# Weight tiles and attention operands moved to other addresses modulo 512 bytes in a one-core encoder block

## The chip, the cores and the metric

One core of a Trainium2 chip runs the whole block in one launch. The metric is the device time of that launch in microseconds. The engines are PE (TensorE: matmuls, with its weight loads listed apart as PEld), DVE (VectorE), ACT (ScalarE), POOL (GpSimd) and SP (SyncE, which issues DMAs here).

## The reference

A hybrid streaming-encoder block on x (1, 512, 1024) and a memory mem (1, 256, 1024), all in float32:

```python
h = rms_norm(x, norm_mix_g)
proj = h @ w_in + b_in
y_a = rwkv7_branch(proj[..., :cb0], ...) @ w_branch_a     # delta-rule recurrence, 8 heads of 64
y_b = rglru_branch(proj[..., cb0:cb1], proj[..., cb1:cb2], ...) @ w_branch_b
merged = sigmoid(proj[..., cb2:cg1]) * y_a + sigmoid(proj[..., cg1:]) * y_b
x = x + merged @ w_mix_out
x = x + cross_attention(rms_norm(x), rms_norm(mem), w_cq, w_ckv, w_co)   # 4 heads of 256
x = x + conv_ffn(rms_norm(x), w_ffn_in, conv, w_ffn_out)                 # d_ff = 2816, causal conv of 3
return rms_norm(x, norm_final_g)
```

## The kernel before, in words

**Three matmuls for one product.** Weights and activations are float32. Each is split into a high part, rounded to the type float32r, and a low part, the rest; a product is high x high, high x low and low x high, summed in PSUM (`mm3`, lines 165 to 169). The weight is always the stationary operand but for the V projection, where the memory is. Line 166 multiplies the high weight with the high activation, line 167 the high weight with the low activation, line 168 the low weight with the high activation. PE loads the weight anew for each of the three.

**Weight tiles.** Weights come from DRAM in tiles of 128 partitions x 1024 float32, that is eight units of 128 x 128. SP issues the load of a tile into a raw tile (tag `wr`, four buffers), ACT casts it to the high part (tag `wh`, three buffers), DVE subtracts to get the low part (tag `wl`, three buffers). `stream` (lines 100 to 122) does so for the dense layers, `stream_quarters` (124 to 135) for the first FFN layer, `out_weights` (1315 to 1343) for the second. Each of them allocates `wh` first and `wl` second.

**Stages, in the order of PE's work.** K projection of the memory (`k_ps`, 256 columns), V projection (`v_ps`), the input projection in 38 blocks (`in_ps`, 512 columns), interleaved with the chunked recurrence of small matmuls; the two branch outputs (`yb_ps`, `ya_ps`, four units a block and eight blocks each), the mix (`mix_ps`), the queries (`q_ps`) interleaved with the attention (`sc_ps`, `prT_ps`, `o_ps`), its output (`co_ps`); then the FFN in a form that needs seven products of half size in place of eight (quarters A11, s1, s2, s4, s3, A12, A22, each 256 columns wide). FFN in runs 11 blocks x 7 products x 2 tiles of 128 rows x 4 units (`fx_ps`, `fyz_ps`); FFN out runs 7 products x 4 rows of tiles x 11 units (`ox_ps`, `oyz_ps`). The sums of weight quarters that this form needs are made by accumulating DMAs on POOL's queue (lines 482 and 518), paced by PE.

**Where the tiles lie.** An address here is a tile's byte offset within a partition, as the program allocates it. Pools lie behind one another. The weight pool comes first, at 16,512: four raw tiles, three high, three low, 4,096 bytes each. The constant pool `cp` follows at 57,472, with `ones` (float32) and `onesr` (float32r) among its tiles, 512 bytes each; then the pool `big` at 65,984, which holds most activations; then, from 115,136, the pools of each stage. Since a unit of weights has 512 bytes and a slice of an activation 1,024 or 2,048, every slice of a tile has the remainder modulo 512 that the tile has:

| tile | role | address mod 512 |
|---|---|---|
| raw, high and low weights | loaded; stationary (moving in the V projection) | 128 |
| h, merged, branch outputs, FFN operands | moving | 448 |
| m2 (the memory) | moving for K, stationary for V | 448 |
| o2 (attention output) | moving for `co_ps` | 0 |
| K2, probabilities prT | moving in the attention | 0 |
| q2, V2 | stationary in the attention | 0 |

The pool `pb` starts with `rxc` and `nrx` (four floats each, 32 bytes taken each: lines 1056 and 1057), which puts o2 behind them at 0 modulo 512 (line 1068).

**The start.** DVE fills `ones` (line 209) and casts it to `onesr` (line 212); eleven matmuls on `onesr` (line 288) wake PE. `ones` serves the float32 sums of squares (lines 271, 338, 1062, 1394), `onesr` the split ones.

**Order.** Weight loads are issued by SP in the order of use, as buffers come free; a high-priority block puts the casts ahead of other work on ACT and DVE. `rxc`, the per-row scale of the scores, is made by `rsqrt` and `newton` (lines 1063 to 1066) from `ssx`, and read by the Exp of the scores (line 1116).

Of the kernel before, what the change touches and what calls it, by code (L numbers as in the profile page):

```python
# [9 lines left out]
F32 = mybir.dt.float32  # L10
F32R = mybir.dt.float32r
# [6 lines left out]
P = 128  # L18
T = 512
D = 1024  # L20
KB = D // P
NMEM = 256
# [36 lines left out]
def hybrid_block_kernel(ctx: ExitStack, tc: tile.TileContext, xT_d, mT_d, pv_d, cst_d, win_d, wk_d, wv_d,  # L59
                        lup_d, gup_d, rga_d, rgx_d, wba_d, wbb_d, wmix_d, wq_d, wo_d, wfi_d, wfo_d, out_d):  # L60
    nc = tc.nc
    V, S, PE = nc.vector, nc.scalar, nc.tensor

    wp = ctx.enter_context(tc.tile_pool(name="wp", bufs=3))
    cp = ctx.enter_context(tc.tile_pool(name="cp", bufs=1))
# [12 lines left out]
    def rw_ps(name, pool=None, tag="rw", **kw):  # L78
        return (pool or prw).tile([P, T], F32, tag=tag, name=name, **kw)
# [16 lines left out]


    wdma, mdma, casts = [], [], []

    def stream(dram, name, between=None, order=None):  # L100

        for g in order or range(dram.shape[0]):
            with tc.high_priority():
                raw = wp.tile([P, 1024], F32, tag="wr", name=f"{name}_r{g}", bufs=4)
                n = 512 if len(wdma) < 2 else 1024
                ins = nc.sync.dma_start(raw, dram[g])
                if between is not None:
                    tc.keep_in_program_order(ins)
                    between(0)
                elif len(wdma) == 1:  # L110
                    tc.add_manual_dep(ins.ins, mdma[-1].ins.name, mybir.DependencyInfo(
                        mybir.DependencyClass.NoSync, mybir.DependencyReason.DATA), reason="order of the loads")
                wdma.append(ins)
                hi = wp.tile([P, 1024], F32R, tag="wh", name=f"{name}_h{g}")
                lo = wp.tile([P, 1024], F32R, tag="wl", name=f"{name}_l{g}")
                for o in range(0, 1024, n):
                    casts.append(S.copy(hi[:, o:o + n], raw[:, o:o + n]))  # L117
                    V.tensor_tensor(lo[:, o:o + n], raw[:, o:o + n], hi[:, o:o + n].bitcast(F32), ALU.subtract)  # L118
                    if between is not None and o == 0:
                        between(1)  # L120
                between = None
            yield hi, lo

    def stream_quarters(srcs, name):

        for g, src in enumerate(srcs):
            with tc.high_priority():
                raw = wp.tile([P, 2, T], F32, tag="wr", name=f"{name}_r{g}", bufs=4)
                wdma.append(nc.sync.dma_start(raw, src))
                hi = wp.tile([P, 2, T], F32R, tag="wh", name=f"{name}_h{g}")  # L130
                lo = wp.tile([P, 2, T], F32R, tag="wl", name=f"{name}_l{g}")
                S.copy(hi, raw)  # L132
                V.tensor_tensor(lo, raw, hi.bitcast(F32), ALU.subtract)  # L133
            for i in range(2):
                yield hi[:, i], lo[:, i]

    class Units:
# [10 lines left out]
        def next(self):  # L148
            if self.left == 0:
                self.fill()  # L150
            i = self.i
            self.i += 1
            self.left -= 1
            return self.hi[:, i * P:(i + 1) * P], self.lo[:, i * P:(i + 1) * P]
# [50 lines left out]


    eps = cp.tile([P, 4], F32, name="eps")
    ones = cp.tile([P, P], F32, name="ones")
    V.memset(ones, 1.0)
    bonesr = cp.tile([P, P], F32R, name="bonesr")  # L210
    onesr = cp.tile([P, P], F32R, name="onesr")
    V.tensor_copy(onesr, ones)
    V.memset(eps[:, 0:1], 1e-6)
    V.memset(eps[:, 1:2], 64e-5)
    V.memset(eps[:, 2:3], 1e-30)
# [67 lines left out]
    with tc.tile_pool(name="p0", bufs=1, reuse_waits="tile") as p0:  # L283
# [103 lines left out]
        for hf in range(2):  # L387
            pss = [(mm_ps if hf else rw_ps)(f"v_ps{hf}_{i}") for i in range(2)]
            for k2 in range(4):
                wh, wl = next(st)  # L390
# [108 lines left out]
    def out_units(m, r, c):  # L499

        return [divmod(((r - 1) * MQ + m) * FB + (c - 1) * HB + k, 8) for k in range(HB)]
# [236 lines left out]
    with tc.tile_pool(name="pz", bufs=1, reuse_waits="tile") as pz:  # L738
# [9 lines left out]
        for s in range(30, -1, -1):  # L748
            n = 31 - s
# [303 lines left out]

    pb_ctx = ExitStack()
    pb = pb_ctx.enter_context(tc.tile_pool(name="pb", bufs=1, reuse_waits="tile"))
    rxc = pb.tile([P, 4], F32, name="rxc")
    nrx = pb.tile([P, 4], F32, name="nrx")
    pat_ctx = ExitStack()
    pat = pat_ctx.enter_context(tc.tile_pool(name="pat", bufs=1, space=PSUM, reuse_waits="tile"))
    psc = rw_ps("rxc_ps", pat, "sc", bufs=2)  # L1060
# [4 lines left out]
    V.tensor_scalar(rxc, rxc, 1.0 / 16, None, ALU.mult)  # L1065
    V.tensor_scalar(nrx, rxc, -1.0, None, ALU.mult)

    o2 = pb.tile([P, 2, KB, T], F32R, name="o2")
    pk_ctx = ExitStack()
    pk = pk_ctx.enter_context(tc.tile_pool(name="pk", bufs=1, reuse_waits="tile"))  # L1070
    K2 = pk.tile([P, 2, KB, NMEM], F32R, name="K2")
    V2 = pk.tile([P, 2, 2, D], F32R, name="V2")

    def load_kv(what, i):
        kv = pk.tile([P, D], F32, tag="kv", name=f"kv{what}{i}", bufs=KVB)
        if what == "K":
            ks = slice(4 * i, 4 * i + 4)
            hi, lo = K2[:, 0, ks], K2[:, 1, ks]
            kv = kv.rearrange("p (m n) -> p m n", n=NMEM)
# [19 lines left out]
        return q2  # L1099

    def attend(hd, q2):
        prT = pk.tile([P, 2, 2, T], F32R, tag="prT", name=f"prT{hd}", bufs=2)
        prps = [rw_ps(f"prT_ps{hd}_{i}", pat, "prT", bufs=2) for i in range(2)]
        for tt in range(4):
            sl = slice(tt * P, (tt + 1) * P)
            ps = rw_ps(f"sc_ps{hd}_{tt}", pat, "sc", bufs=2)
            for i in range(2):
                kb = 2 * hd + i
                PE.matmul(ps[:, :NMEM], q2[:, 0, i, sl], K2[:, 0, kb, :], start=(i == 0), stop=False)
                PE.matmul(ps[:, :NMEM], q2[:, 0, i, sl], K2[:, 1, kb, :], start=False, stop=False)  # L1110
                PE.matmul(ps[:, :NMEM], q2[:, 1, i, sl], K2[:, 0, kb, :], start=False, stop=(i == 1))
            st = pk.tile([P, 4], F32, tag="smst", name=f"smst{hd}_{tt}", bufs=4)
            V.tensor_reduce(st[:, 0:1], ps[:, :NMEM], AX.X, ALU.max)
            V.tensor_tensor(st[:, 1:2], st[:, 0:1], nrx[:, tt:tt + 1], ALU.mult)
            ex = pk.tile([P, NMEM], F32, tag="ex", name=f"ex{hd}_{tt}", bufs=3)
            S.activation(ex, ps[:, :NMEM], AF.Exp, scale=rxc[:, tt:tt + 1], bias=st[:, 1:2],
                         accum_out=st[:, 2:3])
            V.reciprocal(st[:, 3:4], st[:, 2:3])
            V.tensor_scalar(ex, ex, st[:, 3:4], None, ALU.mult)
            for i in range(2):  # L1120
                PE.transpose(prps[i][:, sl], ex[:, i * P:(i + 1) * P], ident)
        for i in range(2):
            S.copy(prT[:, 0, i, :], prps[i])
            V.tensor_tensor(prT[:, 1, i, :], prps[i], prT[:, 0, i, :].bitcast(F32), ALU.subtract)
        for i in range(2):
            kb = 2 * hd + i
            ps = rw_ps(f"o_ps{kb}", pat, "o")
            for n in range(2):
                cs = slice(kb * P, (kb + 1) * P)
                mm3(ps, V2[:, 0, n, cs], V2[:, 1, n, cs], prT[:, 0, n, :], prT[:, 1, n, :], n == 0, n == 1)  # L1130
            S.copy(o2[:, 0, kb, :], ps)
            V.tensor_tensor(o2[:, 1, kb, :], ps, o2[:, 0, kb, :].bitcast(F32), ALU.subtract)
# [36 lines left out]
    for m in order:  # L1169
# [3 lines left out]
        h = ph.tile([P, T], F32, tag=f"h{m // 4}", name=f"h{m}")  # L1173
        S.activation(h, xr[:, m, :], AF.Identity, scale=par("nffn", m))
        i = m % 4
# [139 lines left out]
    def out_weights():  # L1315

        flat = []
        for n in ("A11", "A12", "s1", "s2", "s3", "A22", "s4"):
            for m, k in out_order:
                if n[0] == "A":  # L1320
                    p, i = out_units(m, int(n[1]), int(n[2]))[k]
                    flat.append((p, wfo_d[p], i))
                else:
                    flat.append(((n, m), dO["s2" if n == "s4" else n, m], k))
        for g in range(0, len(flat), 8):
            units = flat[g:g + 8]
            n = len(units) * P
            with tc.high_priority():
                raw = wp.tile([P, 1024], F32, tag="wr", name=f"wfo_r{g // 8}", bufs=4)
                k = 0  # L1330
                while k < len(units):
                    key, src, i = units[k]
                    e = k
                    while e < len(units) and units[e][0] == key and units[e][2] == i + e - k:
                        e += 1
                    nc.sync.dma_start(raw[:, k * P:e * P], src[:, i * P:(i + e - k) * P])
                    k = e
                hi = wp.tile([P, 1024], F32R, tag="wh", name=f"wfo_h{g // 8}")
                lo = wp.tile([P, 1024], F32R, tag="wl", name=f"wfo_l{g // 8}")
                S.copy(hi[:, :n], raw[:, :n])  # L1340
                V.tensor_tensor(lo[:, :n], raw[:, :n], hi[:, :n].bitcast(F32), ALU.subtract)  # L1341
            for k in range(len(units)):
                yield hi[:, k * P:(k + 1) * P], lo[:, k * P:(k + 1) * P]
# [186 lines left out]
```

## Time and profile before

| what | value |
|---|---|
| median of 3 runs | 894.85 us (892.56 to 897.15) |
| span of the profiled execution | 892.8 us |
| mean granted TensorE clock | 0.996 |
| PE busy | 877.4 us, 6197 matmul records |
| weight loads busy | 767.9 us |
| DVE busy | 685.2 us |
| ACT busy | 513.6 us |
| moved by DMA | 201.37 MB |

A row of the timeline has the start in us from the span's start, the duration in us, the engine, the line, the operation, output and inputs, and the shape. Matmuls are pipelined: the duration is the latency of one, and the next starts long before it ends, so a rate is read from starts. A row of waits names who waited, for whom, the total, how often, and the longest. A row of the windows view has, for a stretch of time, the sum and the busy time (and count) of PE, PEld, DVE, ACT and POOL, then the granted clock, the share of the DMA engines and GB/s.

### The profile page before, as it was taken

What the parts mean: (1) busy time and instruction counts of PE and PEld (TensorE: products, weight loads), DVE (VectorE), ACT (ScalarE), POOL (GpSimd) and SP (SyncE); (2) the same over time, 40 slices, a digit from 0 to 9 for tenths busy, and PEclk for the clock granted to TensorE, in tenths of its full rate; (3) what the DMA queues carried; (4) which work ended last, traced back from release to release, by engine and by line L of the source; (5) the groups of instructions that cost most, each with busy time, mean ns of one, the idle gap of its engine ahead of it and who ended that gap; (6) DMA issues with size and microseconds to landing.
All of it is one profiled execution on the core that took longest, in us unless ns stands there. A gap on an engine that the chain in (4) does not pass through costs nothing.

```text
span 892.8 us, 15934 instructions
## 1 busy us (share of the span) xinstructions
PE 877.4 (98%) x6197; PEld 767.9 (86%) x6197; DVE 685.2 (77%) x1104; ACT 513.6 (58%) x783; POOL 132.5 (15%) x163
## 2 busy tenths in 40 slices
PE   8999999999999999999999999999999999999996
PEld 7878878888877677888888778999999999999996
DVE  6796598777967677675575578889888889999674
ACT  6575676634347676233554466766655656757563
POOL 0101222021102021001122111111111111211100
PEclk9999999999999999999999999999999999999999
DMA  7878899678997279758888958999999999998963
GB/s 268 307 253 215 206 228 233 187 203 233 262 227 156 72 203 249 220 166 229 218 234 183 197 137 185 260 275 271 265 255 294 263 297 275 244 276 220 261 202 94
DMA packets 97242, 201.37 MB, mean 226 GB/s; under 512 B 19536, under 2 KB 30928, under 8 KB 97104
## 3 DMA queue, kind: packets, MB, share of 16 engines
q1 hardware_dynamic: 62240, 118.57, 40.4%
q0 software_dynamic: 25504, 67.38, 36.9%
q10 hardware_dynamic: 9424, 14.42, 4.7%
q8 instruction: 48, 0.79, 0.4%
q14 instruction: 26, 0.21, 0.1%
HBM read 188.54 MB, written 78.12 MB: 299 GB/s over the span
## 4 chain that ended last, share of the span: by engine, by line
PE 91%; DVE 4%; DMA 2%; ACT 1%; issue 1%; DVEq 0%; ACTq 0%; SPq 0%
PE in_ps L167 7%; PE in_ps L166 7%; PE in_ps L168 7%; PE fx_ps L167 5%; PE fx_ps L166 5%; PE fx_ps L168 5%; PE fyz_ps L167 4%; PE fyz_ps L166 4%; PE fyz_ps L168 3%; PE ox_ps L166 2%; PE oyz_ps L166 2%; PE ox_ps L168 2%; PE oyz_ps L168 2%; PE oyz_ps L167 2%; PE ox_ps L167 2%; PE co_ps L167 2%
## 5 line engine op out<-in xcount | busy, mean ns | idle before, releaser
L132 ACT CAST wfi_h<-wfi_r 128x1024 fp32r<-128x1024 f32 x77 | 81.1, 1053 | 71.5 <-PE fx_ps L167 19.7
L168 PE MATMUL in_ps<-hT,win_l 128*128 128x512 f32 x304 | 121.3, 399 | 0.0
L167 PE MATMUL in_ps<-hT,win_h 128*128 128x512 f32 x304 | 121.0, 398 | 0.2 <-DVE hT L384 0.2
L166 PE MATMUL in_ps<-hT,win_h 128*128 128x512 f32 x304 | 120.6, 398 | 0.3 <-DVE pr L586 0.3
L133 DVE TENSOR_TENSOR wfi_l<-wfi_r,wfi_h 128x1024 fp32r<-128x1024 f32 x77 | 94.1, 1222 | 22.7 <-ACT wfi_h L132 22.4
L482 POOL DMA_DIRECT2D dS<-in_wfi x66 | 66.7, 1028 | 293.1 <-PE in_ps L166 102.3
L167 PEld LDWEIGHTS in_ps<-hT,win_h 128*128 128x128 f32 x304 | 57.1, 188 | 14.2 <-issue 0.7
L166 PEld LDWEIGHTS in_ps<-hT,win_h 128*128 128x128 f32 x304 | 57.1, 188 | 13.2 <-DVE pr L586 0.7
L168 PEld LDWEIGHTS in_ps<-hT,win_l 128*128 128x128 f32 x304 | 57.1, 188 | 13.1 <-issue 0.7
L518 POOL DMA_DIRECT2D dOs<-in_wfo x54 | 39.8, 784 | 181.5 <-PE fyz_ps L166 54.0
L118 DVE TENSOR_TENSOR win_l<-win_r,win_h 128x1024 fp32r<-128x1024 f32 x38 | 46.3, 1221 | 24.2 <-ACT win_h L117 20.7
L117 ACT CAST win_h<-win_r 128x1024 fp32r<-128x1024 f32 x38 | 39.9, 1050 | 41.1 <-PE in_ps L167 32.4
L1341 DVE TENSOR_TENSOR wfo_l<-wfo_r,wfo_h 128x1024 fp32r<-128x1024 f32 (+1 forms) x39 | 47.2, 1209 | 15.2 <-ACT wfo_h L1340 15.2
L1340 ACT CAST wfo_h<-wfo_r 128x1024 fp32r<-128x1024 f32 (+1 forms) x39 | 40.5, 1039 | 31.3 <-DMA wfo_r<-dOs 11.6
L168 PE MATMUL ox_ps<-go,wfo_l 128*128 128x256 f32 x176 | 49.1, 279 | 0.8 <-DVE wfo_l L1341 0.8
L166 PE MATMUL ox_ps<-go,wfo_h 128*128 128x256 f32 x176 | 49.2, 279 | 0.4 <-ACT wfo_h L1340 0.3
L166 PE MATMUL fx_ps<-hq,wfi_h 128*128 128x256 f32 x176 | 49.4, 280 | 0.0
L166 PE MATMUL fyz_ps<-hq,wfi_h 128*128 128x256 f32 x176 | 49.2, 280 | 0.0
L167 PE MATMUL fx_ps<-hq,wfi_h 128*128 128x256 f32 x176 | 49.2, 280 | 0.0
L167 PE MATMUL fyz_ps<-hq,wfi_h 128*128 128x256 f32 x176 | 49.2, 280 | 0.0
L167 PE MATMUL fx_ps<-hr,wfi_h 128*128 128x256 f32 x176 | 49.2, 280 | 0.0
L166 PE MATMUL fx_ps<-hr,wfi_h 128*128 128x256 f32 x176 | 49.2, 279 | 0.0
(432 smaller groups left out, 2704.9 us busy)
## 6 DMA issues: line engine op xcount, KB each, us to landing
dS<-in_wfi POOLq DMA_DIRECT2D x66, 512.0 KB, 7.8
wfi_r<-dS SPq DMA_DIRECT2D x44, 512.0 KB, 6.8
win_r<-in_win SPq DMA_DIRECT2D x38, 512.0 KB, 5.3
wfi_r<-in_wfi SPq DMA_DIRECT2D x33, 512.0 KB, 5.8
dS<-dS POOLq DMA_DIRECT2D x22, 512.0 KB, 5.7
dOs<-in_wfo POOLq DMA_DIRECT2D x12, 512.0 KB, 7.9
wk_r<-in_wk SPq DMA_DIRECT2D x8, 512.0 KB, 5.1
wv_r<-in_wv SPq DMA_DIRECT2D x8, 512.0 KB, 4.0
```

What stands on the lines that cost most here:

```text
L117: casts.append(S.copy(hi[:, o:o + n], raw[:, o:o + n]))
L118: V.tensor_tensor(lo[:, o:o + n], raw[:, o:o + n], hi[:, o:o + n].bitcast(F32), ALU.subtract)
L132: S.copy(hi, raw)
L133: V.tensor_tensor(lo, raw, hi.bitcast(F32), ALU.subtract)
L166: first = PE.matmul(ps, lh, rh, start=start, stop=False, **kw)
L167: PE.matmul(ps, lh, rl, start=False, stop=False, **kw)
L168: PE.matmul(ps, ll, rh, start=False, stop=stop, **kw)
L482: return lambda: nc.gpsimd.dma_start(s(out), src, **kw)
L518: yield lambda k=k, w=w, src=src: nc.gpsimd.dma_start(dO[n, m][:, k * P:(k + w) * P], src, **kw)
L1340: S.copy(hi[:, :n], raw[:, :n])
L1341: V.tensor_tensor(lo[:, :n], raw[:, :n], hi[:, :n].bitcast(F32), ALU.subtract)
```

## The change

The three places that allocate a high and a low weight tile call a new function, which allocates the low tile first. Three pads are put into the weight pool: 128 bytes ahead of the raw tiles, 128 bytes between the low and the high tiles, 256 bytes behind the high ones. Raw tiles then lie at 256, low parts at 256, high parts at 384 modulo 512, and the pools behind start 512 bytes later.

`ones` is no longer a tile of its own: it is `onesr` read as float32, and DVE writes 1.0 straight into it. The constant pool is 512 bytes shorter, so `big` and all behind it lie where they were.

In the attention o2 is the first tile of its pool, K2 and the two buffers of probabilities follow, and `rxc` and `nrx` become slices of one tile behind them. o2, K2 and the probabilities then lie at 448 modulo 512, V2 and q2 at 0 as before.

No instruction of the loops is added or taken away; one cast at the start goes.

```diff
+    wp.tile([P, 32], F32, name="pad_r", bufs=1)
+    pads = iter(((32, "pad_h"), (64, "pad_e")))
+
+    def weight_tiles(name, g):
+
+        t = {}
+        for i in "lh":
+            t[i] = wp.tile([P, 1024], F32R, tag=f"w{i}", name=f"{name}_{i}{g}")
+            for n, pad in islice(pads, 1):
+                wp.tile([P, n], F32, name=pad, bufs=1)
+        return t["h"], t["l"]
...
-                hi = wp.tile([P, 1024], F32R, tag="wh", name=f"{name}_h{g}")
-                lo = wp.tile([P, 1024], F32R, tag="wl", name=f"{name}_l{g}")
+                hi, lo = weight_tiles(name, g)
...
-                hi = wp.tile([P, 2, T], F32R, tag="wh", name=f"{name}_h{g}")
-                lo = wp.tile([P, 2, T], F32R, tag="wl", name=f"{name}_l{g}")
+                hi, lo = (t.rearrange("p (n f) -> p n f", n=2) for t in weight_tiles(name, g))
...
-    ones = cp.tile([P, P], F32, name="ones")
-    V.memset(ones, 1.0)
     bonesr = cp.tile([P, P], F32R, name="bonesr")
     onesr = cp.tile([P, P], F32R, name="onesr")
-    V.tensor_copy(onesr, ones)
+    ones = onesr.bitcast(F32)
+    V.memset(ones, 1.0)
...
-    rxc = pb.tile([P, 4], F32, name="rxc")
-    nrx = pb.tile([P, 4], F32, name="nrx")
+    o2 = pb.tile([P, 2, KB, T], F32R, name="o2")
+    pk_ctx = ExitStack()
+    pk = pk_ctx.enter_context(tc.tile_pool(name="pk", bufs=1, reuse_waits="tile"))
+    K2 = pk.tile([P, 2, KB, NMEM], F32R, name="K2")
+
+    def probs(hd):
+        return pk.tile([P, 2, 2, T], F32R, tag="prT", name=f"prT{hd}", bufs=2)
+
+    prT0 = probs(0)
+    rxn = pk.tile([P, 16], F32, name="rxn")
+    rxc, nrx = rxn[:, 0:4], rxn[:, 4:8]
...
-    o2 = pb.tile([P, 2, KB, T], F32R, name="o2")
-    pk_ctx = ExitStack()
-    pk = pk_ctx.enter_context(tc.tile_pool(name="pk", bufs=1, reuse_waits="tile"))
-    K2 = pk.tile([P, 2, KB, NMEM], F32R, name="K2")
     V2 = pk.tile([P, 2, 2, D], F32R, name="V2")
...
-        prT = pk.tile([P, 2, 2, T], F32R, tag="prT", name=f"prT{hd}", bufs=2)
+        prT = probs(hd) if hd else prT0
...
-                hi = wp.tile([P, 1024], F32R, tag="wh", name=f"wfo_h{g // 8}")
-                lo = wp.tile([P, 1024], F32R, tag="wl", name=f"wfo_l{g // 8}")
+                hi, lo = weight_tiles("wfo", g // 8)
```

## The prediction

> **What bounds the kernel now.** I read the page's busy times, slices and chain first, then the waits of PE, then the timeline of PE and of its weight loads in seven stretches.
>
> ```profile
> span 892.8 us, 15934 instructions
> PE 877.4 (98%) x6197; PEld 767.9 (86%) x6197; DVE 685.2 (77%) x1104; ACT 513.6 (58%) x783; POOL 132.5 (15%) x163
> PEclk9999999999999999999999999999999999999999
> PE 91%; DVE 4%; DMA 2%; ACT 1%; issue 1%; DVEq 0%; ACTq 0%; SPq 0%
> ```
>
> PE is busy for 98% of the span at the full clock and makes 91% of the chain that ended last. It is hardly ever kept waiting:
>
> ```profile
> PE k_ps L166 <- ACT wk_h L117: 2.3, 1, 2.3
> PE wake L288 <- DVE Pp L616: 1.3, 1, 1.3
> PE ox_ps L168 <- DVE wfo_l L1341: 0.8, 1, 0.8
> ```
>
> So the time is the number of matmuls times the distance from one start to the next. That distance is the point. Here are the first and the last matmul of long unbroken runs (start, duration, line, operands):
>
> ```profile
> 57.41 0.40 PE L166 MATMUL in_ps<-hT,win_h 128*128 128x512 f32 x1
> 66.28 0.40 PE L167 MATMUL in_ps<-hT,win_h 128*128 128x512 f32 x1
> ...
> 215.03 0.39 PE L167 MATMUL in_ps<-hT,win_h 128*128 128x512 f32 x1
> 254.86 0.39 PE L167 MATMUL in_ps<-hT,win_h 128*128 128x512 f32 x1
> ...
> 46.22 0.39 PE L166 MATMUL v_ps<-wv_h,m 128*128 128x512 f32 x1
> 56.95 0.39 PE L167 MATMUL v_ps<-wv_l,m 128*128 128x512 f32 x1
> ...
> 520.00 0.39 PE L168 MATMUL co_ps<-o,wo_l 128*128 128x512 f32 x1
> 551.74 0.39 PE L166 MATMUL co_ps<-o,wo_h 128*128 128x512 f32 x1
> ```
>
> From the first to the last there are 38 steps in the first pair, 174 in the second, 46 in the third, 136 in the fourth: 8.87/38 = 233.4 ns, 39.83/174 = 228.9 ns, 10.73/46 = 233.3 ns, 31.74/136 = 233.4 ns. And for 256 columns:
>
> ```profile
> 600.03 0.28 PE L166 MATMUL fx_ps<-hq,wfi_h 128*128 128x256 f32 x1
> 600.03 0.19 PEld L167 LDWEIGHTS fx_ps<-hq,wfi_h 128*128 128x128 f32 x1
> 639.96 0.28 PE L166 MATMUL fx_ps<-hq,wfi_h 128*128 128x256 f32 x1
> ...
> 843.00 0.28 PE L167 MATMUL ox_ps<-go,wfo_h 128*128 128x256 f32 x1
> 867.28 0.47 PE L166 MATMUL oyz_ps<-go,wfo_h 128*128 128x256 f32 x1
> ...
> 869.54 0.28 PE L166 MATMUL oyz_ps<-go,wfo_h 128*128 128x256 f32 x1
> 883.44 0.28 PE L167 MATMUL oyz_ps<-go,wfo_h 128*128 128x256 f32 x1
> ```
>
> Steps: 339, 214 and 118, so 117.8, 113.5 and 117.8 ns. The second 256 columns of a matmul cost 228.9 - 117.8 = 111.1 ns. The next weight load starts together with the matmul (600.03 in both rows), so the two operands are read side by side, and the cost comes in steps of some 4.4 ns a matmul: 233.3 against 228.9, 117.8 against 113.5.
>
> What goes with the steps? With distance = (moving address minus weight address) mod 512, the in_ps runs have 448 - 128 = 320, v_ps has 128 - 448, that is 192, and co_ps 0 - 128, that is 384. Distance 320 gives 228.9 for most of the kernel; 192 and 384 give 233.3 throughout. But 320 also gave 233.4 for the 38 steps before 66.28, and the 117.8 and 113.5 stretches have one and the same distance, 320: after the wait at 842 PE ran in the better state until its next interruption at 867, then fell back. I read this as two streams that lock into a repeating pattern, with several patterns per address pair, chosen by how the run begins and kept for hundreds of matmuls.
>
> **The change part by part.**
>
> *Weights at 384 (high) and 256 (low).* No instruction is added to the loops. The three matmuls of a product now have distances 64, 64 and 192 in place of 320 three times. The trace shows 192 (233.3 in v_ps, which is a price above today's) and does not show 64, so both sides must be bounded: the dearest shown is 233.3 (+4.4 ns on 512 columns), and on the cheap side the row that is nearest is the better 256-column state: 113.5 - 117.8 = -4.3 ns there, and for 512 columns 113.5 + 111.1 = 224.6 ns, also -4.3. I take -4.3 ns a matmul on 256 columns and, by the step of 233.3 - 228.9, -4.4 on 512: one step down in both shapes. The reason: with high and low parts at one address modulo 512 every matmul repeats its predecessor, and a costly pattern holds until PE is interrupted; with 128 bytes between them the phase is shifted twice in each triple, and the state of 113.5 shows that the better pattern is within reach of the same reads. That reason is argued, not shown; hence the rivals.
>
> The counts, by rows and by the loops:
>
> ```profile
> L168 PE MATMUL in_ps<-hT,win_l 128*128 128x512 f32 x304 | 121.3, 399 | 0.0
> L168 PE MATMUL co_ps<-o,wo_l 128*128 128x512 f32 x64 | 25.3, 398 | 0.0
> 552.00:772.00 220.00, 220.00 (x1854) 219.15 (x1853) 192.79 (x264) 138.22 (x203) 35.86 (x49) 1.00 0.94 268
> ```
>
> - FFN in: 11 blocks x 7 products x 2 x 4 x 3 = 1848 matmuls (the window counts 1854 with its edges): 1848 x 4.3 = 7.9 us.
> - FFN out: 4 x 11 x 7 x 3 = 924, less the 214 that already run at 113.5: 710 x 4.3 = 3.1 us.
> - K projection: 8 x 8 x 3 = 192: 0.8 us.
> - 512 columns: in_ps 3 x 304 = 912 less the 38 of the first pair, wbb and wba 96 each, wmix and wq 192 each, together 1450: x 4.4 = 6.4 us.
> - The V projection (96 matmuls) has the weight tiles as moving operand; its distances become 448 and 320 in place of 192; one step either way is 0.4 us: taken as 0.
>
> *o2, K2 and the probabilities at 448.* co_ps leaves distance 384 for the one that all the others have: 3 x 64 = 192 matmuls from 233.4 to 224.5: 1.7 us. Scores and values, 96 + 48 matmuls, have weights at 0 (q2, V2): 0 +- 0.6 us.
>
> Sum: 7.9 + 3.1 + 0.8 + 6.4 + 1.7 = 19.9 us. PE is on the path for 91% of the span, and around the chunk recurrence and the attention its runs are short; I count nine tenths: 18 us.
>
> *One copy of the ones.*
>
> ```profile
> 1.05 0.23 DVE L212 CAST onesr<-ones 128x128 fp32r<-128x128 f32 x1
> 1.33 4.01 PEld L288 LDWEIGHTS wake<-onesr 128*128 128x128 f32 x11 [1.33 <-DVE Pp L616]
> 8.07 0.39 PE L166 MATMUL k_ps<-m,wk_h 128*128 128x256 f32 x1 [2.29 <-ACT wk_h L117]
> ```
>
> The cast's 0.23 us goes, the waking matmuls can start that much earlier, and they end over 2 us ahead of the first real one, which waits for ACT: 0. If that cover were gone it would be 0.23 us.
>
> *The attention pools reordered.* rxn lies behind K2 and the probabilities, so what it must wait for is another old tile.
>
> ```profile
> 440.10 0.27 ACT L227 ACTIVATE rxc<-rxc_ps,eps 128x4 f32<-128x4 f32 x1 [1.28 <-PE rxc_ps L1062]
> 449.40 0.28 PE L1109 MATMUL sc_ps<-K,q 128*128 128x256 f32 x1
> ```
>
> rxc is written at 440.1, and the first scores, behind which its first reader comes, start at 449.4: over 9 us of cover. Queued behind the Ln on ACT are the weight casts of wq, which run 441.8 on. No DMA changes its queue. Cost 0; a wait that outlasted the cover would cost what it outlasts.
>
> *Will the weights arrive in time?* In FFN in, the DMA engines are busy at 0.94, and PE would take a tile 3.7% faster.
>
> ```profile
> SPq L129 <- DVE wfi_l L133: 116.4, 50, 3.2
> ACT wfi_h L132 <- DMA wfi_r<-in_wfi: 12.5, 4, 4.1
> ```
>
> The load queue waits 116.4 us for buffers that DVE frees, so there the loads are paced by the consumers; casts wait 12.5 us for a load, and PE none. A share of 1.00 would allow 0.06 x 220 = 13 us, more than the 7.9 wanted. DVE, at 192.79 of 220, has room too.
>
> **The rivals.**
>
> *Deeper (0.13).* 512 columns go two steps down, to 220: another 1642 x 4.4 = 7.2 us, 27.1 x 0.9 = 24 us: 870. Against it: no 512-column run in the trace is below 228.9. If 256 columns go another step too, 2750 x 4.4 x 0.9 = 11 us more: 859.
>
> *Half of it (0.17).* Only the 256-column loops gain (11.8 x 0.9 = 11 us: 884), only the 512-column ones (8.1 x 0.9 = 7 us: 887.5), or the weights' supply gives the 7.9 us of FFN in back (885).
>
> *The other side, a dearer pattern (0.15).* The low parts sit at distance 192, where v_ps pays 233.3 in every one of its 46 steps. If the low parts' load sets the pattern of the triple, 512 columns go one step up, 1450 x 4.4 = 6.4, and 256 columns one step, 2750 x 4.4 = 12.1, to 122: 18.5 x 0.9 = 17 us: 911.5; with 512 columns alone, 900.5. It decides from the point where a wmix run, which nothing interrupts, is above 228.9 ns. Against it: the matmuls of v_ps keep one distance all through, the new triples don't.
>
> *No effect (0.13).* The steps are set by how runs begin and not by addresses; then only co_ps moves, by 0 to 2 us: 893.5. For it stand the two rates at distance 320; against it, that every run at 192 or 384 is at 233.3 and nearly every one at 320 is at 228.9. [...]
>
> **How the numbers follow.** The profiled execution's span is 892.8 us, 2 us below the median of the three runs, 894.85 (892.56 to 897.15); I take the 18 us off the median: 876.5 us, chance 0.42, with a range of its own from 872 to 884 (from an eighth above the whole 19.9 us down to half of it). Faster by over 0.5%, about what a measurement of this kernel can tell from no change (below 890.4): 0.42 + 0.13 + 0.17 = 0.72. Within 0.5%: 0.13. Slower: 0.15. The range from 862 to 901 leaves out most of the dearer pattern, 0.11, and the far end of the deeper one, 0.05.
>
> **What would show it.** Right: a wmix run at some 224.5 ns a step with the pattern repeating every three matmuls, co_ps at the same rate as wmix, FFN in at 113.5 (its 1848 matmuls in some 210 us rather than 218), PE's waits still a few microseconds in all. Wrong in the main step: wmix at 228.9 (no effect) or 233 (dearer), whatever the total. Wrong in the cover: PE waits for wfi_h or wfi_l by more than 2 us, or the load queue's waits for buffers shrink while casts wait for DMA. The wake-up and rxc should stay off the chain that ended last.

## The result and the profile after

The changed kernel takes 898.16 us (median of six executions, 896.44 to 900.64) beside 894.06 us for the kernel before on the same chip: a ratio of 1.0046, 95% interval 1.0029 to 1.0064. It is slower by 0.3 to 0.6%, where 2% faster was forecast. The first profiled execution ran 44 matmuls of `mix_ps` from 800 to 820 us, 0.455 us each, where the kernel before has 191 of them in 43.4 us, 0.227 us each, and it took 1731.88 us; it is left out, and the profile after is that of another run of the same kernel (run e1, 895.81 us in that execution).

The page of the kernel after, lines that answer to those of before:

```profile
span 894.0 us, 15935 instructions
PE 879.3 (98%) x6197; PEld 768.9 (86%) x6197; DVE 685.2 (77%) x1103; ACT 513.5 (57%) x783; POOL 132.6 (15%) x163
PE 90%; DVE 4%; DMA 2%; ACT 2%; issue 1%; DVEq 0%; ACTq 0%
```

PE is as busy as before and still makes nine tenths of the chain. Its waits (who, for whom, us, times, longest), the three largest:

```profile
PE k_ps L175 <- ACT wk_h L127: 2.4, 1, 2.4
PE prT_ps L1134 <- DVE ex L1132: 1.4, 1, 1.4
PE wake L296 <- DVE Pp L624: 1.1, 1, 1.1
```

One of them is new, 1.4 us in the first attention head. The steps, from the timeline, first and last matmul of unbroken runs:

```profile
186.24 0.39 PE L175 MATMUL in_ps<-hT,win_h 128*128 128x512 f32 x1
256.45 0.40 PE L177 MATMUL in_ps<-hT,win_l 128*128 128x512 f32 x1
...
347.93 0.39 PE L177 MATMUL yb_ps<-yb,wbb_l 128*128 128x512 f32 x1
438.89 0.40 PE L175 MATMUL q_ps<-hx,wq_h 128*128 128x512 f32 x1
...
521.12 0.40 PE L177 MATMUL co_ps<-o,wo_l 128*128 128x512 f32 x1
555.00 0.39 PE L177 MATMUL co_ps<-o,wo_l 128*128 128x512 f32 x1
...
581.63 0.28 PE L176 MATMUL fx_ps<-hq,wfi_h 128*128 128x256 f32 x1
607.26 0.28 PE L177 MATMUL fx_ps<-hr,wfi_l 128*128 128x256 f32 x1
607.66 0.28 PE L176 MATMUL fx_ps<-hr,wfi_h 128*128 128x256 f32 x1
786.11 0.28 PE L177 MATMUL ox_ps<-go,wfo_l 128*128 128x256 f32 x1
```

The counts are 301, 397, 148, 226 and 1501 steps, so 233.3, 229.1, 228.9, 113.4 and 118.9 ns. The forecast was 224.5 for 512 columns and 113.5 for 256. The long in_ps run went up from 228.9, co_ps came down from 233.4, wmix and its neighbours stayed. In this execution, 1.2 us longer than the one before the change, in_ps costs 1.7 us more and the attention 1.9, of which 1.4 are the new wait; the start is 1.6 us shorter. The two last pairs are the telling ones: one loop, one set of addresses, and at an interruption at 607.4 PE goes from a step of 113.4 ns to 118.9 and keeps that for 1501 matmuls, dearer than the 117.8 of before.

By stage, from the first matmul of each in the timelines (us, each rounded; e10 and e11 are further executions of the changed kernel, told below; e8 and e12 one other layout):

```
                          before    e1   e10   e11 |   e8   e12
start to first in_ps        57.4  55.8  59.3  57.0 | 57.2  56.2
in_ps to first yb_ps       288.8 290.5 290.7 291.1 |287.9 287.9
yb_ps to first score       103.2 103.3 105.0 104.9 |102.4 102.3
first score to co_ps        53.1  55.0  54.2  52.9 | 54.4  53.2
co_ps to first fx_ps        51.3  50.7  50.7  51.4 | 50.4  50.4
fx_ps to first ox_ps       218.8 219.2 214.4 220.6 |214.1 211.1
ox_ps to the end           120.2 119.6 121.3 118.8 |118.4 119.0
span                       892.8 894.0 895.7 896.6 |884.8 880.1
```

### The profile page after: what moved, and what is told of

Read it like the earlier page. It is cut to its first block, busy times and chain, and to the rows that moved or that the text cites. A ratio compares the mean times of both kernels' runs of the same rounds, so it can differ in the third digit from the quotient of the medians.

```text
span 1730.1 us, 15935 instructions
## 1 busy us (share of the span) xinstructions
PE 1719.8 (99%) x6197; PEld 1366.8 (79%) x6197; DVE 699.4 (40%) x1103; ACT 519.9 (30%) x783; POOL 132.7 (8%) x163
## 4 chain that ended last, share of the span: by engine, by line
PE 99%; DMA 0%; ACT 0%; DVE 0%; DVEq 0%; issue 0%
PE in_ps L177 8%; PE in_ps L176 8%; PE in_ps L175 8%; PE fx_ps L175 5%; PE fx_ps L176 5%; PE fx_ps L177 5%; PE fyz_ps L177 4%; PE fyz_ps L176 4%; PE fyz_ps L175 4%; PE ox_ps L176 2%; PE ox_ps L175 2%; PE ox_ps L177 2%; PE oyz_ps L176 2%; PE oyz_ps L175 2%; PE oyz_ps L177 2%; PE q_ps L176 2%
## 5 line engine op out<-in xcount | busy, mean ns | idle before, releaser
L177 PE MATMUL in_ps<-hT,win_l 128*128 128x512 f32 x304 | 208.0, 684 | 0.0
L176 PE MATMUL in_ps<-hT,win_h 128*128 128x512 f32 x304 | 207.0, 681 | 0.0
L175 PE MATMUL in_ps<-hT,win_h 128*128 128x512 f32 x304 | 205.9, 679 | 0.0
L177 PEld LDWEIGHTS in_ps<-hT,win_l 128*128 128x128 f32 x304 | 91.3, 300 | 49.9 <-issue 46.2
L175 PEld LDWEIGHTS in_ps<-hT,win_h 128*128 128x128 f32 x304 | 90.5, 298 | 49.5 <-issue 45.0
L176 PEld LDWEIGHTS in_ps<-hT,win_h 128*128 128x128 f32 x304 | 89.0, 293 | 50.9 <-issue 46.8
L177 PE MATMUL fyz_ps<-hq,wfi_l 128*128 128x256 f32 x176 | 77.6, 441 | 0.0
L175 PE MATMUL fx_ps<-hr,wfi_h 128*128 128x256 f32 x176 | 77.5, 441 | 0.0
L175 PE MATMUL fx_ps<-hq,wfi_h 128*128 128x256 f32 x176 | 77.5, 441 | 0.0
L176 PE MATMUL fx_ps<-hr,wfi_h 128*128 128x256 f32 x176 | 77.4, 440 | 0.0
L176 PE MATMUL ox_ps<-go,wfo_h 128*128 128x256 f32 x176 | 77.3, 439 | 0.0
L175 PE MATMUL ox_ps<-go,wfo_h 128*128 128x256 f32 x176 | 77.3, 439 | 0.0
L176 PE MATMUL fyz_ps<-hq,wfi_h 128*128 128x256 f32 x176 | 77.3, 439 | 0.0
L177 PE MATMUL ox_ps<-go,wfo_l 128*128 128x256 f32 x176 | 77.3, 439 | 0.0
L175 PE MATMUL fyz_ps<-hq,wfi_h 128*128 128x256 f32 x176 | 77.1, 438 | 0.0
```

The costliest lines, as they stand in the source:

```text
L175: first = PE.matmul(ps, lh, rh, start=start, stop=False, **kw)
L176: PE.matmul(ps, lh, rl, start=False, stop=False, **kw)
L177: PE.matmul(ps, ll, rh, start=False, stop=stop, **kw)
```

## The experiments

**The two halves of the change, alone.** e1 is the changed kernel again; e2 has its weight addresses and the attention tiles of before; e3 has its attention tiles and the weights at 128.

```diff
+    rxc = pb.tile([P, 4], F32, name="rxc")
+    nrx = pb.tile([P, 4], F32, name="nrx")
     o2 = pb.tile([P, 2, KB, T], F32R, name="o2")
...
-    rxn = pk.tile([P, 16], F32, name="rxn")
-    rxc, nrx = rxn[:, 0:4], rxn[:, 4:8]
```

(e2 against the changed kernel; e3 is the attention part of the change put on the kernel before.)

> The changed kernel once more, for an undisturbed profile. [...] Theory 2 (rival): rates are as before (228.9 and 117.8) and the 4 us come from somewhere else, such as new waits in the attention or the weight supply; PE's waits are then longer by some 4 us. Time 898 us either way.

> Weights at 384 and 256, the attention's tiles where they were before (o2, K2, probabilities at 0). Theory 1: co_ps has distances 128, 128 and 256 in its triple and its own rate; the rest as in the changed kernel; 895 to 902 us. Theory 2: if the attention's new places cause the loss, this one is as fast as before, 894 us.

> Weights at 128 as before, o2, K2 and the probabilities at 448. Theory 1: co_ps goes from 233.4 to 228.9 ns, 192 matmuls, 0.9 us faster: 893 us. Theory 2: 4 us slower than before, 898 us.

Measured: e1 897.13 us, ratio 1.0032 (1.0014 to 1.0049); e2 897.1 us, 1.0031 (1.0007 to 1.0056); e3 894.42 us, 1.0002 (0.9986 to 1.0018). The loss comes with the weights' addresses; the attention tiles make no difference that the time can show. Theory 2 of e1 does not hold: the FFN ran at 118.9 ns for most of its length, not at 117.8, and the largest new wait of PE is 1.4 us, not 4. e2's profile has no such wait in the attention and is still 3.2 us longer than the one before the change: in_ps takes 291.2 us and FFN in 220.1. In e3's profile co_ps runs at 229.0 ns, as theory 1 said, and its stage takes 50.7 us in place of 51.3, too little to be seen in the time. The single copy of the ones was never run alone; it is part of e2.

**Matmuls alone, by address.** e4 runs nothing but matmuls, eight high by eight low addresses, in the kernel's triples.

```python
for u in range(REP):
    rh, rl = mov(u % 3, n), mov(3 + u % 3, n)
    PE.matmul(ps[:, :n], unit(0, hi, u), rh, start=u == 0, stop=False)
    PE.matmul(ps[:, :n], unit(0, hi, u), rl, start=False, stop=False)
    PE.matmul(ps[:, :n], unit(2048 - 128, lo, u), rh, start=False, stop=u == REP - 1)
```

> Leaves the whole block out: a kernel of matmuls alone. For each of the 8 x 8 pairs of addresses of high and low weights (multiples of 64 modulo 512), with the moving operand at 448, 16 triples as in the kernel, first with 512 columns and then with 256, each stretch of 48 begun afresh after a wait. Theory 1: the rates differ from pair to pair in steps of some 2.2 ns; 128 and 128 give 228.9 and 117.8 (or 233.3 and 113.5), 384 and 256 a rate that is not lower in both shapes. Theory 2: all pairs give one rate per shape.

Mean step of the last 30 of 48 matmuls, ns, the moving operand at 448 (rows: high address, columns: low address, mod 256):

```
512 columns      0      64     128    192 | 256 columns    0      64     128    192
high   0       233.3  231.1  231.8  233.3 |              113.3  118.2  113.3  117.8
high  64       230.0  232.2  233.3  233.3 |              118.7  120.0  120.0  118.4
high 128       233.5  233.8  228.9  228.9 |              118.9  115.5  117.8  117.4
high 192       231.1  231.1  231.8  226.7 |              117.8  119.1  117.9  120.0
```

The table shows the cells with both addresses below 256. With 512 columns, moving an address by 256 bytes changes no cell by more than 0.4 ns. With 256 columns that is so in twelve of the sixteen; the other four (64/0, 64/64, 64/128 and 128/0) change by 0.9 to 5.6 ns when the low part moves by 256 bytes. The addresses set the step here, with PE busy for 92% of e4's span, ACT for 6% and DVE for 0%, and the kernel's values are in the table: 228.9 and 117.8 at 128/128, as before. The change's pair, 384/256, had 233.2 with 512 columns; with 256 it had 113.3, but 118.9 stood in the cell that is the same modulo 256. The best of the table are 226.7 and 113.3, and no one pair has both.

**Distance, or address? And one pattern, or several?** e5 moves weights and moving operand together, then begins stretches in five ways; e9 was to run ten blocks behind one another with a single odd matmul between them.

```python
for r in range(0, 256, 64):
    for mv in range(0, 256, 64):
        stretch(f"a{n}w{r}m{mv}", n, r, r, mv)
...
for lead in (0, 64, 128, 192, 320):
    stretch(f"b{n}h{hi}l{lo}c{lead}", n, hi, lo, lead=lead)
```

> This kernel leaves the whole block out; it runs matmuls alone, 48 to a stretch in triples (high weight twice, low weight once), and its output is not the block's. Part A: one weight address for both parts at 0, 64, 128, 192 mod 256 bytes, and the moving operand at 0, 64, 128, 192 mod 256. Part B: five weight pairs (high 384 low 256; 128 128; 0 0; 192 192; 0 128), moving at 448, each begun with no extra matmul or with one of 64, 128, 192 or 320 columns just ahead. Part C: one weight address at 16, 32, 96, 160, 224 and 240. Theory A (what counts is the distance from the weight's address to the moving operand's, modulo 256 bytes): in part A all four cells of one distance agree within 0.5 ns, with 512 columns 226.7 at distance 0, 228.9 at 64, 232.2 at 128, 233.3 at 192, and with 256 columns 120.0, 117.8 or 115.5, 120.0 and 113.3. Rival B (the absolute addresses count): cells of one distance differ by over 2 ns. On the beginnings, theory C (the same addresses have several steady patterns, and how a stretch begins picks one): for 384/256 at 256 columns the five beginnings give both 113.3 and 118.9; rival D (one pattern per pair, the two values in the kernel came from what ran between): the five beginnings agree within 0.5 ns.

In e5 all other engines are all but idle (page of e5):

```profile
PE 824.7 (91%) x4576; PEld 699.9 (78%) x4576; DVE 2.7 (0%) x2; ACT 50.5 (6%) x97; POOL 0.2 (0%) x4
```

Its timeline has, for weights and moving operand both at 0, both at 64, then 0 and 192, and 64 and 0, the first and last of 30 steps each:

```profile
24.14 0.39 PE L54 MATMUL a512w0m<-m,w 128*128 128x512 f32 x1
30.94 0.39 PE L54 MATMUL a512w0m<-m,w 128*128 128x512 f32 x1
...
84.58 0.39 PE L54 MATMUL a512w64m<-m,w 128*128 128x512 f32 x1
91.38 0.39 PE L54 MATMUL a512w64m<-m,w 128*128 128x512 f32 x1
...
60.27 0.39 PE L54 MATMUL a512w0m<-m,w 128*128 128x512 f32 x1
67.27 0.39 PE L54 MATMUL a512w0m<-m,w 128*128 128x512 f32 x1
...
72.46 0.40 PE L54 MATMUL a512w64m<-m,w 128*128 128x512 f32 x1
79.46 0.40 PE L54 MATMUL a512w64m<-m,w 128*128 128x512 f32 x1
```

6.80/30 = 226.7 twice, 7.00/30 = 233.3 twice: the step goes with the distance modulo 256, not with either address. With 512 columns all 16 cells fall in line within 0.2 ns: 226.7 at distance 0, 228.9 at 64, 232.2 at 128, 233.3 at 192. With 256 columns it is 120.0 at 0, 117.8 at 64, 118.7 at 128, 117.8 at 192; two of these missed the expectation (120.0 at 128, 113.3 at 192). In between, the step isn't between: part C has 233.3 with 512 columns at distance 32, and 234.5 at 160, dearer than any multiple of 64. As to beginnings, 384/256 gave 228.9 once and 233.1 to 233.6 four times with 512 columns, and, against the expectation, 118.9 five times with 256; 0/0 at 256 columns gave 113.3 three times and 117.8 twice. So several patterns, but which pair shows them in five trials is luck; hence e9:

```python
for b, lead in enumerate((0, 64, 128, 192, 320, 384, 448, 64, 192, 448)):
    if lead:
        PE.matmul(aux[:, :lead], unit(0, hi, 0), mov(0, lead, MV), start=b == 1, stop=b == 9, skip_group_check=True)
    for u in range(REP):
        ...
```

> This kernel leaves the whole block out and runs matmuls alone. For the weight pairs 384/256 (high/low, mod 512), 128/128 and 256/384, the moving operand at 448, with 512 and with 256 columns: ten blocks of 48 matmuls in triples, one after the other, and between two blocks a single matmul of 64, 128, 192, 320, 384 or 448 columns, with no wait of PE. Theory C (a pair may have several steady patterns, and an interruption alone moves it from one to another): 384/256 shows 228.9 in some blocks and 233.1 to 233.6 in others with 512 columns, and 113.3 and 118.9 with 256, while 128/128 (228.9; 117.8) and 256/384 (231.8; 113.3) stay within 0.5 ns in all ten blocks. Rival D (the pattern is chosen by what other engines and transfers do meanwhile, which this kernel has none of): each pair keeps one value in all ten blocks.

Only the first stretch (384/256, 512 columns) ran so. In the timeline of the others the first three or four odd matmuls stand together ahead of the first block, so the blocks that they were to part are one unbroken run of 192 or 240 matmuls, and a stretch has six or seven runs, not ten. For 384/256 at 256 columns, the last 30 steps of the first run, and of the run behind the next odd matmul (384 columns):

```profile
381.45 0.28 PE L57 MATMUL b256h384l<-m,w 128*128 128x256 f32 x1
384.85 0.28 PE L57 MATMUL b256h384l<-m,w 128*128 128x256 f32 x1
387.15 0.28 PE L57 MATMUL b256h384l<-m,w 128*128 128x256 f32 x1
390.72 0.28 PE L57 MATMUL b256h384l<-m,w 128*128 128x256 f32 x1
```

3.40/30 = 113.3, then 3.57/30 = 119.0 (118.9 from the unrounded starts): here one odd matmul changes the pattern, and it holds till the next. The last 30 steps of every run, in order:

```
512 columns  384/256   228.9 233.6 233.2 233.2 233.5 233.2 228.9 233.6 228.9 233.1
             128/128   228.9 in all six
             256/384   231.8 to 231.9 in all six
256 columns  384/256   113.3 118.9 118.9 113.3 118.9 118.9
             128/128   117.8 in five, 113.3 in two
             256/384   113.3 in all seven
```

Rival D falls with 384/256, and the theory holds but for 128/128 at 256 columns, which has two patterns as well: those of the kernel before, 117.8 and 113.5. The change's pair has two in both shapes, and the dearer is above before's in both. Its mirror image, high at 256 and low at 384, shows one only in these six and seven runs. That does not prove that there is no other: 128/128 with 512 columns gave 228.9 in all eleven runs of e5 and e9, and yet in_ps ran at 233.4 for 38 steps in the kernel before, straight behind v_ps (e3 shows the same).

**The changed kernel, further executions.** e10 is the changed kernel unaltered. e11 was to put the second load of K later:

```diff
-        if hd == 0:
+        if hd == 1:
             load_kv("K", 1)
```

> The changed kernel as it is, once more with a profile. Theory C (the pattern that a stage falls into differs from execution to execution): the FFN's steps are again 113.3 or 118.9 ns and those of in_ps 228.9 or 233.3, but the stretches that have the one and the other lie elsewhere, and the spans of the two executions differ by what their shares make (the FFN in and out together has 2772 matmuls, so a tenth of them changing over is 1.5 us). Rival: the same stretches have the same steps to 0.5 ns in both executions, and the spread of the times comes from waits.

> The changed kernel with the second load of K (its DMA, its cast on ScalarE and its subtraction on VectorE) put behind the second head and not the first. In the changed kernel ScalarE stands 2.0 us before that cast of K (its DMA lands 7.2 us after its issue), the exponentials of the first head queue behind it, and PE waits 1.4 us for ex. Theory: this wait of PE goes, the stage of the attention (the first score matmul to the first of co_ps) is 53 to 54 us and not 55.0, and the time falls by about 1.4 us, to 895.7; the matmul steps stay as they are. Rival (the wait has another cause, or comes back before the third head's scores): 55 us, 897 us.

e10: 897.48 us. Its timeline has these runs of 982 and 397 steps:

```profile
613.53 0.28 PE L176 MATMUL fx_ps<-hr,wfi_h 128*128 128x256 f32 x1
724.84 0.28 PE L177 MATMUL fyz_ps<-hq,wfi_l 128*128 128x256 f32 x1
...
351.68 0.39 PE L177 MATMUL yb_ps<-yb,wbb_l 128*128 128x512 f32 x1
444.27 0.40 PE L175 MATMUL q_ps<-hx,wq_h 128*128 128x512 f32 x1
```

That is 113.4 ns where e1 had 118.9, and 233.2 where e1 had 229.1: the same program. e11, 1729 steps:

```profile
583.91 0.28 PE L176 MATMUL fx_ps<-hq,wfi_h 128*128 128x256 f32 x1
789.46 0.28 PE L177 MATMUL ox_ps<-go,wfo_l 128*128 128x256 f32 x1
```

118.9 again. e11's edit did not do what it says: the planner left the load where it was, and the order on every engine is that of the changed kernel but for buffer numbers. So its 898.77 us (ratio 1.0057, 1.0037 to 1.0076) are the changed kernel once more, and the miss against the expected 895.7 says nothing of K. That PE does not wait for `ex` in e11 shows that this wait comes and goes with the execution. The profiles show what sets it: the second load of K, behind whose cast the exponentials stand on ScalarE. Where ScalarE waits 0 to 0.7 us for that load (e2, e11, before), PE's wait ahead of `prT_ps` is nil; at 0.8 (e3, e12) it is 0.2, at 1.7 to 2.0 (e10, e8, e7, e1) 1.2 to 1.4, at 2.4 (e6) 1.8. Why the load takes longer in some executions stays open.

**Other layouts.** e6 exchanges the two parts; e7 puts both at the moving operands' own address; e8 uses two places in longer weight tiles; e12 is e8 with the edit of e11.

```diff
-        for i in "lh":
+        for i in "hl":
```
```diff
-    wp.tile([P, 32], F32, name="pad_r", bufs=1)
-    pads = iter(((32, "pad_h"), (64, "pad_e")))
+    wp.tile([P, 80], F32, name="pad_r", bufs=1)
+    pads = iter(((48, "pad_e"),))
```
```diff
-    wp.tile([P, 32], F32, name="pad_r", bufs=1)
-    pads = iter(((32, "pad_h"), (64, "pad_e")))
+    wp.tile([P, 16], F32, name="pad_r", bufs=1)
+    pads = iter(((48, "pad_e"),))
...
-            t[i] = wp.tile([P, 1024], F32R, tag=f"w{i}", name=f"{name}_{i}{g}")
+            t[i] = wp.tile([P, 1088], F32R, tag=f"w{i}", name=f"{name}_{i}{g}")
...
-        return t["h"], t["l"]
+        h, l = (16, 48) if name in ("wk", "wfi", "wfo") else (0, 0)
+        return t["h"][:, h:h + 1024], t["l"][:, l:l + 1024]
```

> The change with the two parts exchanged: high parts at 256, low parts at 384 mod 512; nothing else. Theory A (each step is set by the distances from the weights to the moving operand modulo 256 bytes, and the counts price them): 512 columns at 231.8 ns, 256 columns at 113.3 ns throughout. Against the kernel before: 912 matmuls of in_ps x +2.6 and 576 of yb, ya, mix and q x +2.85, 192 of co_ps x -1.4, 96 of v_ps x -1.5: +3.6 us; K 192 x -4.5, FFN in 1848 x -4.5, FFN out 924 x -3.1: -12.0 us; sum -8.4 us, 885 us. Rival B (the change loses because the two parts lie at two addresses, or by its pads and buffers): 896 to 898 us, as the change itself.

> Both parts of the weights at 448 mod 512, the moving operands' own address (distance 0); attention tiles as in the change. Theory A: 512 columns at 226.7 ns: in_ps 912 x -2.6, yb, ya, mix and q 576 x -2.3, co_ps 192 x -6.6, v_ps 96 x -6.6, together -5.6 us; 256 columns at 120.0 ns: K 192 x +2.2, FFN in 1848 x +2.2, FFN out 924 x +3.6, together +7.8 us; sum +2.2 us, 896 us: the fastest dense stages and the slowest FFN of all in one kernel. Rival B (one address for both parts is as good as the kernel before): 894 us with 228.9 and 117.8 ns.

> The weight tiles are 256 bytes longer; stages with 512 columns use both parts at 192 mod 256 (distance 0), K and the FFN use the high part at 0 and the low part at 128 mod 256 (distances 192 and 64); attention tiles as in the change, and two buffers for ex where there were three, to make room. Theory A: 226.7 ns with 512 columns and 113.3 ns with 256: -5.6 us and -12.0 us against the kernel before, 876 us. Rival C (the loads, the casts or VectorE become late once PE is faster): less than half of it, 885 us or more, with new idle time of PE that casts or DMAs end.

> The kernel with two places for the weights (e8) and the second load of K behind the second head, as in e11: the same edit as there, but in a kernel whose address pairs each showed one pattern, so that its 1.3 us are not lost in the choice of patterns. Theory: 512 columns at 226.7 ns and 256 at 113.3 ns throughout; PE's wait of 1.3 us for ex in the first head is gone and the attention's stage is 1.3 us shorter; 885 us, the fastest here. Rival: the time stays at 886 to 888 us, because what PE gains there it waits for later, at casts of weights in the FFN.

e6: 891.72 us, ratio 0.9967 (0.9947 to 0.9988), so two kernels that differ only in which part lies where stand on the two sides of the kernel before. e7: 898.38 us, 1.005 (1.0034 to 1.0066). e8: 886.45 us, 0.990 (0.9868 to 0.9932). e12: 887.08 us, 0.992 (0.9897 to 0.9942); its order on the engines is e8's but for buffer numbers, so it repeats e8, and its shorter wait for `ex` (0.2 us against 1.3) is no work of the edit. The steps came as priced. e7's timeline, 397 and 1876 steps:

```profile
346.94 0.39 PE L177 MATMUL yb_ps<-yb,wbb_l 128*128 128x512 f32 x1
437.01 0.39 PE L175 MATMUL q_ps<-hx,wq_h 128*128 128x512 f32 x1
...
561.78 0.28 PE L177 MATMUL fx_ps<-hq,wfi_l 128*128 128x256 f32 x1
786.90 0.34 PE L175 MATMUL ox_ps<-go,wfo_h 128*128 128x256 f32 x1
```

226.9 and 120.0 ns. e12's, 397 and 1696 steps:

```profile
345.77 0.39 PE L178 MATMUL yb_ps<-yb,wbb_l 128*128 128x512 f32 x1
435.83 0.39 PE L176 MATMUL q_ps<-hx,wq_h 128*128 128x512 f32 x1
...
576.22 0.28 PE L177 MATMUL fx_ps<-hq,wfi_h 128*128 128x256 f32 x1
768.49 0.28 PE L178 MATMUL ox_ps<-go,wfo_l 128*128 128x256 f32 x1
```

226.9 and 113.4 ns. e7 lies 4.5 us above before where +2.2 was priced: its profile has +3.3, of which 1.3 is the wait for `ex` in the attention. e6 has 113.3 ns too, but in its profile, the slowest of its twelve executions (span 897.1 us), FFN in takes 217.6 us where 1848 x 113.3 ns make 209.4. Some 5 us of that are lost in two places: from 690 to 710 us and from 730 to 750 PE ran 155 and 151 matmuls where 20.0/0.1133 = 176 fit; it waited 1.5 us for `wfi_l` and 1.0 for ACT's `p`. Its median gained 2.2 us where 8.4 were expected. And of the 17.6 us that the steps were to give, e8 got 8.0 in its profile (884.8 against 892.8) and 7.4 in its median; e12's profile, the fastest of its six executions, got 12.7 (its median 7.2). In the stage table, e8's FFN in is 4.7 us shorter and e12's 7.7, of the 1848 x 4.5 ns = 8.3 us that were priced. Windows of e8 from 575 us on (sum, busy PE, PEld, DVE, ACT, POOL, clock, DMA share, GB/s):

```profile
575.00:687.00 112.00, 111.75 (x986) 111.55 (x985) 99.27 (x136) 68.55 (x102) 18.66 (x27) 1.00 0.95 279
687.00:700.00 13.00, 11.48 (x91) 10.49 (x90) 12.45 (x17) 8.66 (x15) 1.76 (x3) 1.00 0.97 245
700.00:766.00 66.00, 66.00 (x585) 66.00 (x584) 61.74 (x84) 42.10 (x61) 11.15 (x16) 1.00 0.94 278
```

And its waits in FFN in:

```profile
PE fx_ps L178 <- DVE wfi_l L143: 0.8, 1, 0.8
PE fyz_ps L176 <- ACT p L1283: 0.5, 1, 0.5
```

Between 687 and 700 us PE ran 91 matmuls where 13.0/0.1133 = 115 fit: 24 x 0.113 = 2.7 us lost, with DVE busy 12.45 of 13 and the only wait in FFN in for a low part that DVE makes. In e12 PE waits for no weight there. So rival C of e8 is there in some executions; neither "all" nor "less than half" was right throughout. Where the medians of e8 and e12 lost the rest of the 17.6 us was not traced.

## Why the prediction was wrong

*PE is the bound, and time is matmuls times steps.* Right: PE is busy for 98% of the span as before and makes 90% of the chain (91% before), and the steps of e7 and e12 came as priced (226.9 and 120.0 ns; 226.9 and 113.4), though e8's FFN in became 4.7 us shorter where 8.3 were priced.

*"One step down in both shapes."* This is the step that failed. For a pair not in the trace it took the better state's -4.3 and -4.4 ns, over the shown +4.4 on the other side. The pair has two patterns in each shape: 228.9 or 233.3, and 113.4 or 118.9. In place of -8.1 us in the 512-column stages, in_ps became dearer (288.8 us to 290.5, 290.7 and 291.1) and yb to q the same or dearer; in place of -11.8 us in the K and FFN loops, FFN in went +0.4, -4.4 and +1.8 by the pattern it met, and FFN out -0.6, +1.1 and -1.4. The size of the step had no ground either: e4 has 226.7, 228.9, 230.0, 231.1 and 231.8 among its values, not levels 4.4 ns apart, and no run with 512 columns was faster than 226.7.

*Distance modulo 512.* Half of the reading was right (the distance counts: 226.7 to 233.3 ns in e5), half wrong: with 512 columns no cell of e4 changes by more than 0.4 ns when an address moves by 256 bytes, and with 256 columns twelve of sixteen don't. Taken modulo 256, before's 320 is 64, and the "new" distances 64, 64, 192 keep the high part where it was and move only the low part, to the distance that v_ps had shown at 233.3. The row against the change stood in the prediction and was given a chance of 0.15, to decide by the wmix run. Its matmuls take 228.9 ns in e1, as in the kernel before, and 233.4 in e10 and e11, and the time lies between no effect and the 900.5 us of that rival with 512 columns alone.

*The reason given for it*, that 128 bytes between the parts break a costly pattern, falls: 384/256 itself keeps a costly pattern until it is interrupted (118.9 ns for 1501 matmuls), and its mirror 256/384, with the same 128 bytes between the parts, showed 113.3 in seven runs of seven: the gap alone decides nothing. Several patterns for one pair of addresses, changed at an interruption and kept after it: right, 113.3 and 118.9 ns in e9. Why one pair of addresses has a longer step than another, no run here shows.

*co_ps.* 228.9 in e1 and e10, not 224.5; in e11 it is 233.1, and the stage has 51.4 us, as before. Its 1.7 us was 0.6 in two executions and 0 in the third.

*No effect.* Wrong too: the addresses set the steps in e4 (226.7 to 233.8 ns with 512 columns) and e5 (226.7 to 233.3), and the time is 0.3 to 0.6% above that of before. That beginnings count as well was right: e9 has 113.3 and 118.9 ns at one pair of addresses.

*K and V.* K's 0.8 us came and went in waits: the stages up to in_ps took 55.8, 59.3 and 57.0 us, against 57.4 (in e10 PE waits 3.4 us for `kt`, before 0.8). The V projection, taken as 0, went from 233.3 to 231.3 ns, which is 0.2 us.

*The ones, the attention pools, the supply.* The pools at nothing: right within what e3 can tell. The ones were not run alone; in e1's profile the waking matmuls wait 1.1 us in place of 1.3, and the first real one still waits 2.4 us for ACT, which fits a cost of nothing. The supply held for the changed kernel, whose FFN did not become faster for long; in e8 the faster PE did run into it for 2.7 us, where 13 us of room had been argued for the loads and DVE was said to have room too; there it was busy for 12.45 of 13 us.

## What to carry to other kernels

Where PE never waits, read its step from the starts of the first and last matmul of unbroken runs, stage by stage: here the addresses of weight and moving operand alone moved it from 226.7 to 233.3 ns with 512 columns (e5) and from 113.3 to 120.0 with 256 (e4). Before changing a layout, measure the candidate pairs in a small kernel of matmuls, in the loop's own order and with interruptions, and prefer one that shows a single pattern over many beginnings; a pair with two makes the time a matter of luck (FFN in took 219.2 us in e1 and 214.4 in e10, the same program). See in the timeline that the interruptions are where they were meant to be. Choose for the stage that has the most matmuls, and check that casts and loads can follow the faster PE (e8 lost 2.7 us between 687 and 700 us, with DVE busy for 12.45 of 13).

## What the runs showed of the hardware

- With PE busy for 91% of the span, ACT for 6% and DVE for 0% (e5), both parts of the weight at one address and distances in multiples of 64, the step with 512 columns went with (moving address - weight address) modulo 256 bytes: 226.7 ns at 0, 228.9 at 64, 232.2 at 128, 233.3 at 192, within 0.2 ns in 16 cells. The best distance for 512 columns there, 0, was the worst for 256 (120.0).
- With the high and the low weight at two distances 384/256 had two steady patterns with 256 columns, 113.3 and 118.9 ns, the latter kept for 1501 steps in e1, the one changed to the other by one odd matmul in e9. Two executions of one program differ in them: FFN in took 219.2 us in e1 and 214.4 in e10. With one address for both parts there were two as well: 117.8 and 113.3 (e9, 128/128).
- A version with each stage at its own distance (e8, e12) takes 886.45 and 887.08 us, 0.8 to 1.0% below the kernel before.
